# A hybrid decoder layer: 24 of its 32 gate blocks computed by seven block products in an early stage and kept in DRAM

## The chip, the cores and the metric

One NeuronCore of a Trainium2 chip runs the whole program in one launch. The metric is device time in microseconds of that core, the median of three runs. Engines are called PE (matmul; PEld its weight loads), DVE (vector), ACT (scalar, activations), POOL and SP (here only the queue that issues most DMAs).

## What is computed

A decoder layer on x of 1024 tokens by 1024 features, all in float32. After an RMSNorm, one projection feeds four mixers, each 512 wide: A (HGRN2), B (Mamba-2 SSD), C (GLA) and D (RG-LRU). They are merged with sigmoid gates, which are themselves projections of the normalised input:

```python
xn = rmsnorm(h, norm_mix_w[l]);  proj = xn @ w_in[l]          # mg: the last 4*1024 columns
yd = rglru_branch(lx, lg, ...)                               # conv, two gates, a scan, times gelu(lg)
branch_out = einsum('blnw,nwd->blnd', stack([ya, yb, yc, yd]), w_branch[l])
merged = sum(sigmoid(mg).reshape(b, s, 4, 1024) * branch_out, axis=2)
h = h + merged @ w_out[l]
g_ff, u_ff = split(rmsnorm(h, norm_ffn_w[l]) @ w_ffn_in[l], 2)
out = rmsnorm(h + (silu(g_ff) * u_ff) @ w_ffn_out[l], norm_f_w)
```

## The kernel before

Every float32 operand of a large matmul is split into a high part (type fp32r) and a remainder, and a product is three passes: high by high, high by low, low by high (`mm3`). ACT makes the high part (a cast) and DVE the remainder (a subtraction). The normalised input lies feature-major in `xn[hf][k]`: two token halves of 512, eight feature blocks of 128, each a pair of `half` tiles.

A projection block of 128 columns, `proj(col)`, loads 512 KB of weights, splits them (`load_w`, lines 151 and 152) and makes 8 x 3 matmuls of 512 columns for each token half, 48 in all. A gate block `gate(b, dm)` is such a projection with a tanh behind it (line 370). There are 32 of them, four branches b by eight blocks dm. `branch(b, dm)` multiplies the mixer's output with w_branch, 24 matmuls; DVE then forms (gate + 1) * branch (line 382, twice) and adds it into `merged[dm]` (line 386; not for branch 3, which comes first and whose g tile becomes `merged`). `merge(b, y)` does gate and branch for dm 0 to 7.

The program's order: norm and `split_fm` of both token halves (lines 231 to 235); RG-LRU (lines 425 to 471: projection LX, conv, small gate matmuls at line 431, sqrt at 456, scan at 460, projection LG with gelu at 348, the product at 468, the split of the result at 360 and 361); `values` for A (a token-major projection of 2 x 256 columns); hgrn(0); merge(3); A's four attentions with projections between them; merge(0); C's attention; the SSD, whose eight `chunk`s are called from merge(2), one ahead of each gate block; branch 1's eight gates in a row, then its eight branch products; w_out; the FFN. The FFN's input projection treats two blocks of 128 columns (a "pair") as a 2 x 2 block matrix and computes it by seven block products of 12 matmuls (84 for what would be 96) from sums of weight quarters S1 to S4 and of activation quarters T1 to T4 (lines 1034 to 1050, 1105 to 1108, 1116 to 1144; the T operands are made at lines 963 to 1013).

Large tiles (128 x 1024) come from a pool of 26, `slot`; halves (128 x 512) from a pool of 32, `half`. Weight staging: `wr` (raw), `wh`, `wl` have two buffers each; PSUM has 4 `pd`, 2 `pq` and 2 `pt` banks. A planner puts the instructions of each engine into one fixed order, by program order among those that its own model finds ready; on the chip each engine runs that order strictly. DMA issues of `nc.sync` stand in one such order on SP.

Of the kernel before, what the change touches and what calls it, by code (L numbers as in the profile page):

```python
# [38 lines left out]
P = 128  # L39
# [32 lines left out]
def trunk(ctx: ExitStack, tc: tile.TileContext, x, w_in, w_branch, w_out, w_fin, w_fout, prm_d, gw_d, lw_d,  # L72
# [43 lines left out]
    def f32(t):  # L116
        return t.bitcast(F32)
# [72 lines left out]
    def quad(p):  # L190
        return p.rearrange("p (c v) -> p c v", c=4)
# [30 lines left out]
            V.scalar_tensor_tensor(r, q, 1.5, r, op0=add, op1=mult)  # L222
        return r

    def split_fm(srcs, wcol, bank):

        res = []
        for k in range(KD):
            p = bank()
            for t in range(4):  # L230
                TE.transpose(p[:, t * P:(t + 1) * P], srcs[t][:, k * P:(k + 1) * P], ident)
            h, l = half(F32R), half(F32R)
            wc = pv(wcol, k)
            A.activation(h, p, AF.Copy, scale=wc)
            V.scalar_tensor_tensor(l, p, wc, f32(h), op0=mult, op1=sub)
            res.append((h, l))
            halves.append((h, l))
        return res

    halves = []  # L240

    def norm_x(hf):
        ss = sm.tile([P, 8], F32, name="ss", tag="ss")
# [19 lines left out]
    for hf in range(2):  # L263
        norm_x(hf)
        if hf == 0:
            wlx.append(load_w(None, KD, rlx[0]))
        xn[hf] = split_fm(xt[hf * 4:hf * 4 + 4], "nmix", allbank)
        if hf == 0:
# [12 lines left out]
    slot.free(*xt)  # L281

    def dense_fm(w, act, bank=dense_bank, first=None):

# [138 lines left out]
    cneg = cp.tile([P, 4], F32, name="cneg")  # L423
    rr, bb, th, yd = [], [], [], []
    for i in range(4):
        u = conv(proj(C_LX + i * P, *((wlx[i], first[i]) if i < 2 else ())), [pv("lcw", i * 4 + j) for j in range(4)], pv("lcb", i))
# [184 lines left out]
    def values(w):  # L611

        v = [slot() for _ in range(2)]

        def use(tp, p):
            for j in range(2):
                A.copy(tm(v[j])[:, tp * 2:tp * 2 + 2, :], p[:, :, j * P:(j + 1) * P])

        proj_tm(w, use)
        return v  # L620
# [325 lines left out]

    dp = ctx.enter_context(tc.tile_pool(name="dp", bufs=1, space=bass.MemoryType.DRAM))
# [3 lines left out]
    def two(dt=F32):  # L953
        t = slot(dt)
        return t[:, 0:H], t[:, H:T], t

    KH = KD // 2
    names = ("B11", "B21", "B22", "T1", "T2", "T3", "T4")
    ops = {n: [None] * KH for n in names}
    op_slots, op_halves = [], []  # L960
# [55 lines left out]
    class Pair:
        def __init__(self, j):
            self.j, self.W, self.held = j, {}, []
            graw = load_raw(w_fin[:, j * P:(j + 1) * P], KD)
            uraw = load_raw(w_fin[:, DFF + j * P:DFF + (j + 1) * P], KD)  # L1020
            g2, u2 = (a.rearrange("p (s k) n -> p s (k n)", s=2) for a in (graw, uraw))
            self.quads = g2[:, 0], g2[:, 1], u2[:, 0], u2[:, 1]
            gh, gl = whi(), wlo()
            graw = graw.rearrange("p k n -> p (k n)")
            A.copy(gh, graw)  # L1025
            V.tensor_sub(gl, graw, f32(gh))
            self.W["A11"], self.W["A12"] = (gh[:, 0:H], gl[:, 0:H]), (gh[:, H:T], gl[:, H:T])

        def sums(self, i):

            a11, a12, a21, a22 = self.quads
            x, h, l = slot(), slot(F32R), slot(F32R)
            if i == 0:
                V.tensor_add(x[:, 0:H], a21, a22)
                V.tensor_sub(x[:, H:T], x[:, 0:H], a11)
                self.s2 = x
            else:
                V.tensor_sub(x[:, 0:H], a11, a21)
                V.tensor_sub(x[:, H:T], a12, self.s2[:, H:T])
                slot.free(self.s2)  # L1040
            A.copy(h, x)
            V.tensor_sub(l, x, f32(h))
            for n, c in zip((("S1", "S2"), ("S3", "S4"))[i], (0, H)):
                self.W[n] = h[:, c:c + H], l[:, c:c + H]
            self.held += [h, l]
            if i:
                slot.free(x)
                uh, ul, ut = two(F32R)
                A.copy(uh, a22)
                V.tensor_sub(ul, a22, f32(uh))  # L1050
                self.W["A22"] = uh, ul
                self.held.append(ut)
# [45 lines left out]
    def ffn_in(j, early=False):  # L1098
# [1 line left out]
        pair = pairs.pop(j)  # L1100

        def product(p, a, b, first=True):
            ah, al = (t.rearrange("p (k n) -> p k n", k=KH) for t in pair.W[a])
            for k, (bh, bl) in enumerate(ops[b]):
                TE.matmul(p, lhsT=ah[:, k], rhs=bh, start=first and k == 0, stop=False, skip_group_check=True)  # L1105
                TE.matmul(p, lhsT=ah[:, k], rhs=bl, start=False, stop=False, skip_group_check=True)  # L1106
            for k, (bh, bl) in enumerate(ops[b]):
                TE.matmul(p, lhsT=al[:, k], rhs=bh, start=False, stop=k == KH - 1, skip_group_check=True)  # L1108
# [194 lines left out]
```

## Time and profile before

| | us |
|---|---|
| median of three runs (lowest, highest) | 2051.46 (2050.77, 2053.79) |
| the profiled execution: its own time | 2052.34 |
| its span, first to last instruction | 2050.4 |
| PE busy in the span | 2006.1 |
| DVE busy | 1030.5 |
| ACT busy | 632.9 |
| DMA traffic | 147.56 MB, mean 72 GB/s |

Busy time of PE counts matmuls that overlap in its pipeline, so a full PE is seen better in how many matmuls start per microsecond. The rows below show the stretches that the text speaks of.

### The profile page before, as it was taken

Reading aid. Unit: us, or ns where it says so; the run is one execution under the profiler, and the core shown is the slowest. Engines: PE = TensorE matmul, PEld = TensorE weight load, DVE = VectorE, ACT = ScalarE, POOL = GpSimd, SP = SyncE. Lnnn points to the kernel's source line nnn. Section 1 sums busy time; section 2 is a strip of 40 time slices with the busy share of each in tenths; the row PEclk is TensorE's granted clock in tenths of the full one; section 3 lists DMA queues with packets and bytes.
Section 4 is the critical chain, followed back from the end, with each engine's and each line's share of the span. In section 5 each row is a group of like instructions: output and inputs, shape, how many; then the busy total and the mean of one; then the engine's idle time right before and its main releaser. Section 6 shows DMA issues by size and latency. Waiting matters only on the chain.

```text
span 2050.4 us, 23991 instructions
## 1 busy us (share of the span) xinstructions
PE 2006.1 (98%) x9892; PEld 1663.1 (81%) x9892; DVE 1030.5 (50%) x1728; ACT 632.9 (31%) x942; POOL 14.2 (1%) x20
## 2 busy tenths in 40 slices
PE   7989999999999999999999999999999999999998
PEld 6779888889888878877779888877888888888886
DVE  6560114765242377566562517268665565554532
ACT  5742112332341111442122323154222232243421
POOL 0000000000000000000000000000000000000000
PEclk9999999999999999999999999999999999999999
DMA  5120111111112110111112014122222222466451
GB/s 172 31 72 11 51 52 32 29 46 42 32 32 61 41 32 21 42 42 31 31 43 66 21 52 154 52 93 83 91 64 93 93 64 91 128 205 221 154 165 41
DMA packets 157772, 147.56 MB, mean 72 GB/s; under 512 B 7472, under 2 KB 134880, under 8 KB 157664
## 3 DMA queue, kind: packets, MB, share of 16 engines
q1 hardware_dynamic: 153824, 136.82, 21.9%
q10 hardware_dynamic: 3840, 9.23, 1.2%
q8 instruction: 77, 1.26, 0.3%
q14 instruction: 31, 0.25, 0.0%
HBM read 126.10 MB, written 19.92 MB: 71 GB/s over the span
## 4 chain that ended last, share of the span: by engine, by line
PE 89%; DVE 7%; ACT 2%; issue 1%; DMA 1%; SPq 0%; DVEq 0%; ACTq 0%
PE pd L199 13%; PE pd L200 13%; PE pd L202 13%; PE pd L1106 3%; PE pd L1105 3%; PE pd L1108 3%; PE pd L318 3%; PE pd L316 3%; PE pd L317 3%; PE pd L1202 2%; PE pd L1203 2%; PE pd L1201 2%; PE pq L1108 2%; PE pq L1106 2%; PE pq L1105 2%; PE pt L1105 1%
## 5 line engine op out<-in xcount | busy, mean ns | idle before, releaser
L199 PE MATMUL pd<-x,wh 128*128 128x512 f32 x1056 | 420.1, 398 | 7.4 <-ACT s L348 7.0
L200 PE MATMUL pd<-x,wh 128*128 128x512 f32 x1056 | 418.1, 396 | 0.0
L152 DVE TENSOR_TENSOR wl<-wr,wh 128x1024 fp32r<-128x1024 f32 x82 | 100.4, 1224 | 370.8 <-PE pd L202 264.4
L202 PE MATMUL pd<-x,wl 128*128 128x512 f32 x1056 | 271.9, 394 | 0.0
L199 PEld LDWEIGHTS pd<-x,wh 128*128 128x128 f32 x1056 | 199.4, 189 | 51.8 <-ACT s L348 7.8
L200 PEld LDWEIGHTS pd<-x,wh 128*128 128x128 f32 x1056 | 199.4, 189 | 41.1 <-issue 2.4
L202 PEld LDWEIGHTS pd<-x,wl 128*128 128x128 f32 x1056 | 196.4, 188 | 42.8 <-issue 3.5
L151 ACT CAST wh<-wr 128x1024 fp32r<-128x1024 f32 x82 | 86.3, 1052 | 249.5 <-PE pd L200 227.8
L316 PE MATMUL pd<-s,x 128*128 128x256 f32 (+2 forms) x512 | 159.5, 312 | 0.6 <-ACT s L151 0.6
L318 PE MATMUL pd<-s,x 128*128 128x256 f32 (+2 forms) x512 | 159.8, 312 | 0.0
L317 PE MATMUL pd<-s,x 128*128 128x256 f32 (+2 forms) x512 | 159.6, 312 | 0.0
L370 ACT ACTIVATE s<-pd 128x512 f32<-128x512 f32 x64 | 38.3, 598 | 217.7 <-PE pd L202 217.7
L316 PEld LDWEIGHTS pd<-s,x 128*128 128x128 f32 x512 | 97.4, 190 | 5.7 <-ACT s L151 0.8
L317 PEld LDWEIGHTS pd<-s,x 128*128 128x128 f32 x512 | 97.5, 190 | 5.1
L318 PEld LDWEIGHTS pd<-s,x 128*128 128x128 f32 x512 | 97.5, 190 | 4.8
L199 PE MATMUL pd<-s,wh 128*128 128x512 f32 x256 | 99.8, 390 | 0.0
L200 PE MATMUL pd<-s,wh 128*128 128x512 f32 x256 | 99.8, 390 | 0.0
L382 DVE SCALAR_TENSOR_TENSOR s<-s,pd 128x512 f32<-128x512 f32 x64 | 43.9, 687 | 94.5 <-PE pd L202 94.5
L1159 DVE TENSOR_TENSOR s<-wr,s 128x1024 fp32r<-128x1024 f32 x44 | 53.9, 1225 | 69.0 <-ACT s L1158 54.2
L523 DVE COPY_PREDICATED s<-msk,pq 128x256 f32<-128x256 uint8 x128 | 61.9, 555 | 29.6 <-PE pq L517 16.2
L1025 ACT CAST wh<-wr 128x1024 fp32r<-128x1024 f32 x22 | 23.2, 1055 | 161.7 <-PE pq L1106 79.6
L202 PE MATMUL pd<-s,wl 128*128 128x512 f32 x256 | 68.5, 389 | 0.0
(341 smaller groups left out, 3560.4 us busy)
## 6 DMA issues: line engine op xcount, KB each, us to landing
wr<-in_w_in SPq DMA_DIRECT2D x76, 512.0 KB, 3.6
wr<-in_w_fin SPq DMA_DIRECT2D x44, 512.0 KB, 4.6
wr<-in_w_fout SPq DMA_DIRECT2D x44, 512.0 KB, 3.6
asp<-s SPq DMA_DIRECT2D x22, 512.0 KB, 4.9
x<-asp SPq DMA_DIRECT2D x42, 256.0 KB, 3.9
wr<-in_w_branch SPq DMA_DIRECT2D x16, 512.0 KB, 3.3
s<-in_x SPq DMA_DIRECT2D x8, 512.0 KB, 7.4
wr<-in_w_out SPq DMA_DIRECT2D x8, 512.0 KB, 3.9
```

The source lines that it names most:

```text
L151: i = A.copy(h, raw)
L152: V.tensor_sub(l, raw, f32(h))
L199: TE.matmul(p, lhsT=wh[k], rhs=ah, start=k == 0, stop=False)
L200: TE.matmul(p, lhsT=wh[k], rhs=al, start=False, stop=False)
L202: TE.matmul(p, lhsT=wl[k], rhs=ah, start=False, stop=k == n - 1)
L316: TE.matmul(p, lhsT=ah, rhs=wh, start=k == 0, stop=False)
L317: TE.matmul(p, lhsT=ah, rhs=wl, start=False, stop=False)
L318: TE.matmul(p, lhsT=al, rhs=wh, start=False, stop=k == n - 1)
L523: V.copy_predicated(dst[:, :, :, side, :], m, pv_[ab][:, i].rearrange("p c (n h) -> p c n h", h=h))
L1105: TE.matmul(p, lhsT=ah[:, k], rhs=bh, start=first and k == 0, stop=False, skip_group_check=True)
L1106: TE.matmul(p, lhsT=ah[:, k], rhs=bl, start=False, stop=False, skip_group_check=True)
L1108: TE.matmul(p, lhsT=al[:, k], rhs=bh, start=False, stop=k == KH - 1, skip_group_check=True)
```

## The change

Blocks of branch 3 (dm 0 to 7), branch 0 (dm 0 to 7), branch 2 (dm 4 to 7) and branch 1 (dm 4 to 7), 24 in all, are computed in a new stage `gates_phase` directly after `split_fm`, as 12 pairs by the FFN's scheme (class `Pair` and `block_product`, moved up and made general). Their tanh is stored to DRAM tiles `gsp`, and `gate` loads it from there. The stage also computes the four LX projections (kept in DRAM as `lxsp`) and makes the activation sums T1 to T4; `split_fm` of the second token half writes an unsplit copy of each feature block as well. Four feature blocks of the second half are given up during the stage (their unsplit copies lie in `xsp`), and are loaded and split again at its end. The RG-LRU comes after the stage and loads LX; A's two `values` calls stand between its blocks. `merge` may load up to three stored gates ahead while a slot is free.

```diff
 def split_fm(srcs, wcol, bank, raws=None):
             A.activation(h, p, AF.Copy, scale=wc)
             V.scalar_tensor_tensor(l, p, wc, f32(h), op0=mult, op1=sub)
+            if raws:
+                A.activation(raws[k], p, AF.Copy, scale=wc)
 def gate(b, dm):
         t = slot()
+        if (b, dm) in gsp:
+            nc.sync.dma_start(t, gsp[b, dm])
+            return t
 def merge(b, y, also=None):
+        gs = []
         for dm in range(KD):
             if also:
                 also(dm)
-            g = gate(b, dm)
+            while not gs or ((b, dm) in gsp and len(gs) < 3 and dm + len(gs) < KD and slot.held < slot.n):
+                gs.append(gate(b, dm + len(gs)))
             if dm % 2 == 0:
                 load_br(b, dm)
-            branch(b, dm, as_act(y), g, V)
+            branch(b, dm, as_act(y), gs.pop(0), V)
+    EARLY = ((3, 0), (0, 0), (2, 4), (1, 4))
+    gsp = {(b, dm): dp.tile([P, T], F32, ...) for b, dm0 in EARLY for dm in range(dm0, KD)}
+    def gates_phase():
+        def use(i, ps):
+            xx = in_order(ps)
+            nc.sync.dma_start(lxsp[i], xx)
+            slot.free(xx)
+        for i in range(2):
+            use(i, proj(0, wlx[i], first[i]))
+        ops = {"B11": xn[0][0:KH], "B21": xn[0][KH:], "B22": xn[1][KH:]}
+        left = [two() for k in range(KH)]
+        for k in range(KH):
+            nc.sync.dma_start(xsp[k], right[k][0])
+            V.tensor_add(b11, f32(h), f32(l))
+            V.tensor_sub(b11, b12, b11)
+            split("T1", k, b11)
+        use(2, proj(C_LX + 2 * P))
...
+        use(3, proj(C_LX + 3 * P))
+        prepare(0, 0)
...
+        for q in range(len(blocks) // 2):
+            prepare(q + 1, 0)
+            pair = pairs.pop(q)
+            pa, pb, pc, pd = (sbank(), tbank(), sbank(), tbank()) if q % 2 else (dense_bank() for i in range(4))
+            u = tmp()
+            g = [[half() for _ in range(2)] for _ in range(2)]
+            def done(i, hf, src):
+                A.activation(g[i][hf], src, AF.Tanh, scale=0.5)
+                nc.sync.dma_start(gsp[blocks[2 * q + i]][:, hs(hf)], g[i][hf])
+            product(pa, "A11", "B11")
+            A.copy(u, pa)
+            product(pd, "S1", "T1")
+            product(pb, "S2", "T2")
+            V.tensor_add(u, u, pb)
+            slot.free(*pair.held[0:2])
+            prepare(q + 1, 1)
+            product(pc, "S3", "T3")
+            V.tensor_add(g[1][1], u, pc)
+            V.tensor_add(g[1][1], g[1][1], pd)
+            done(1, 1, g[1][1])
+            product(pa, "A12", "B21", False)
+            done(0, 0, pa)
+            product(pc, "A22", "T4", False)
+            V.tensor_add(g[1][0], u, pc)
+            done(1, 0, g[1][0])
+            product(pd, "S4", "B22", False)
+            V.tensor_add(u, u, pd)
+            done(0, 1, u)
+        for k in range(KH):
+            r = tmp()
+            nc.sync.dma_start(r, xsp[k])
+            h, l = xn[1][k] = half(F32R), half(F32R)
+            A.copy(h, r)
+            V.tensor_sub(l, r, f32(h))
+    gates_phase()
     lw = slot()
     nc.scalar.dma_start(lw, lw_d)
+    wv = w_tm(C_HI)
+    va = []
     for i in range(4):
-        u = conv(proj(C_LX + i * P, ...), ...)
+        xx = slot()
+        nc.sync.dma_start(xx, lxsp[i])
+        u = conv(xx, ...)
...
         A.activation(th[i], r, AF.Tanh, scale=cpos[:, i:i + 1])
+        if i % 2 == 0:
+            va += values(wv)
+            if i == 0:
+                wv = w_tm(C_HI + 256)
...
-    va = []
-    for i in range(2):
-        w = wv
-        if i == 0:
-            wv = w_tm(C_HI + 256)
-        va += values(w)
     nxt = hgrn(0)
     merge(3, yd)
```

## Rows read from the trace of the kernel before

**Rows 1.** The page: span, and busy time of the engines with its share.

```profile
span 2050.4 us, 23991 instructions
PE 2006.1 (98%) x9892; PEld 1663.1 (81%) x9892; DVE 1030.5 (50%) x1728; ACT 632.9 (31%) x942; POOL 14.2 (1%) x20
```

**Rows 2.** Windows (start:end length, busy us per engine): merge(3), merge(0), FFN in, FFN out.

```profile
200.00:320.00 120.00, 120.00 (x531) 99.34 (x531) 23.48 (x27) 20.70 (x27) 0.00 (x0) 1.00 0.18 49
...
600.00:700.00 100.00, 100.00 (x443) 82.81 (x442) 26.55 (x28) 16.67 (x21) 0.00 (x0) 1.00 0.18 50
1400.00:1750.00 350.00, 350.00 (x1544) 289.76 (x1545) 218.63 (x292) 104.61 (x140) 0.00 (x0) 1.00 0.27 85
1800.00:1950.00 150.00, 150.00 (x663) 124.22 (x662) 76.31 (x112) 59.28 (x88) 0.00 (x0) 1.00 0.62 200
```

**Rows 3.** Chain that ended last, in time: one projection's two halves in merge(3).

```profile
240.55 1.81 PE pd L202 x8
245.99 1.81 PE pd L202 x8
```

**Rows 4.** Groups of DVE instructions in the FFN's input stage, 1400 to 1750.

```profile
L1042 DVE TENSOR_TENSOR s<-s 128x1024 fp32r<-128x1024 f32 x38 | 46.5, 1222 | 8.9 <-ACT s L1041 8.9
L1139 DVE TENSOR_TENSOR s<-s,t 128x512 f32<-128x512 f32 x19 | 13.1, 692 | 2.1 <-DVE t L1138 0.5
```

**Rows 5.** Windows at the end of the RG-LRU (columns as in Rows 2; then clock).

```profile
101.00:106.50 5.50, 3.79 (x17) 2.86 (x16) 5.50 (x5) 5.44 (x7) 0.00 (x0) 1.00 0.00 0
117.40:122.70 5.30, 0.05 (x1) 0.00 (x0) 4.19 (x5) 1.58 (x3) 0.00 (x0) 0.87 0.00 0
122.70:128.00 5.30, 5.29 (x13) 4.13 (x14) 4.19 (x6) 2.48 (x4) 0.00 (x0) 0.50 0.00 0
```

**Rows 6.** Timeline there: ACT and PE, with the idle time before each.

```profile
121.11 1.04 ACT L360 CAST s<-s 128x1024 fp32r<-128x1024 f32 x1 [9.48 <-DVE s L468]
...
122.71 0.80 PE L199 MATMUL pd<-x,wh 128*128 128x512 f32 x1 [5.26 <-ACT s L348]
```

**Rows 7.** Timeline of ACT in the second half's split_fm: first two of eight.

```profile
30.93 0.69 ACT L234 ACTIVATE x<-pt,prm 128x512 fp32r<-128x512 f32 x1 [3.54 <-PE pt L231]
31.52 0.68 ACT L234 ACTIVATE x<-pd,prm 128x512 fp32r<-128x512 f32 x1
```

**Rows 8.** Window in the FFN's operand preparation and first pairs.

```profile
1385.00:1395.00 10.00, 7.60 (x28) 4.52 (x27) 10.00 (x17) 3.07 (x6) 0.00 (x0) 1.00 0.00 1
```

**Rows 9.** DMA issues: KB of each, median us from issue to landing.

```profile
wr<-in_w_fout SPq DMA_DIRECT2D x44, 512.0 KB, 3.6
...
wr<-in_w_branch SPq DMA_DIRECT2D x16, 512.0 KB, 3.3
s<-in_x SPq DMA_DIRECT2D x8, 512.0 KB, 7.4
```

**Rows 10.** Timeline of DVE ahead of merge(0) and in it.

```profile
584.38 2.91 DVE L625 SCALAR_TENSOR_TENSOR s<-pt,prm,s 128x512 f32<-128x512 f32 x4
587.21 2.55 DVE L361 TENSOR_TENSOR s<-s 128x1024 fp32r<-128x1024 f32 x2
...
634.26 0.69 DVE L382 SCALAR_TENSOR_TENSOR s<-s,pd 128x512 f32<-128x512 f32 x1 [2.10 <-PE pd L202]
634.99 1.23 DVE L386 TENSOR_TENSOR s<-s 128x1024 f32<-128x1024 f32 x1
```

**Rows 11.** Windows of merge(2): chunks 4, 5, 6 with 7, the tail, one chunk.

```profile
1006.50:1029.30 22.80, 22.80 (x106) 17.10 (x105) 13.49 (x22) 3.69 (x6) 0.00 (x0) 1.00 0.16 47
1029.30:1052.10 22.80, 22.80 (x106) 17.24 (x105) 12.56 (x21) 4.30 (x6) 0.00 (x0) 1.00 0.08 24
1052.10:1075.20 23.10, 23.10 (x112) 16.65 (x111) 17.29 (x29) 6.62 (x10) 0.00 (x0) 1.00 0.17 46
1075.20:1097.00 21.80, 21.80 (x100) 18.09 (x99) 7.58 (x10) 3.19 (x4) 0.00 (x0) 1.00 0.17 49
...
961.00:976.00 15.00, 15.00 (x71) 10.90 (x72) 11.58 (x20) 1.97 (x4) 0.00 (x0) 1.00 0.13 35
```

More of the change, by code (lines that the diff above doesn't have):

```diff
@@ L223, in rstd_of, with split_fm @@
         return r
-    def split_fm(srcs, wcol, bank):
+    def split_fm(srcs, wcol, bank, raws=None):
         res = []
@@ L235, in split_fm, with two @@
             V.scalar_tensor_tensor(l, p, wc, f32(h), op0=mult, op1=sub)
+            if raws:
+                A.activation(raws[k], p, AF.Copy, scale=wc)
             res.append((h, l))
-            halves.append((h, l))
         return res
-    halves = []
+    dp = ctx.enter_context(tc.tile_pool(name="dp", bufs=1, space=bass.MemoryType.DRAM))
+    KH = KD // 2
+    def two(dt=F32):
+        t = slot(dt)
+        return t[:, 0:H], t[:, H:T], t
     def norm_x(hf):
@@ L266, in trunk @@
             wlx.append(load_w(None, KD, rlx[0]))
-        xn[hf] = split_fm(xt[hf * 4:hf * 4 + 4], "nmix", allbank)
-        if hf == 0:
+        if hf:
+            right = [two() for k in range(KH)]
+            xn[1] = split_fm(xt[4:8], "nmix", allbank, [right[k % KH][k // KH] for k in range(KD)])
+        else:
+            xn[0] = split_fm(xt[0:4], "nmix", allbank)
+            slot.free(*xt[0:4])
             wlx.append(load_w(None, KD, rlx[1]))
@@ L280, in trunk @@
     slot.free(mskf)
-    slot.free(*xt)
+    slot.free(*xt[4:8])
     def dense_fm(w, act, bank=dense_bank, first=None):
@@ L414, in conv, with __init__, sums @@
         return u
+    class Pair:
+        def __init__(self, w, c0, c1):
+            self.W, self.held = {}, []
+            graw = load_raw(w[:, c0:c0 + P], KD)
+            uraw = load_raw(w[:, c1:c1 + P], KD)
+            g2, u2 = (a.rearrange("p (s k) n -> p s (k n)", s=2) for a in (graw, uraw))
+            self.quads = g2[:, 0], g2[:, 1], u2[:, 0], u2[:, 1]
+            gh, gl = whi(), wlo()
+            graw = graw.rearrange("p k n -> p (k n)")
+            A.copy(gh, graw)
+            V.tensor_sub(gl, graw, f32(gh))
+            self.W["A11"], self.W["A12"] = (gh[:, 0:H], gl[:, 0:H]), (gh[:, H:T], gl[:, H:T])
+        def sums(self, i):
+            a11, a12, a21, a22 = self.quads
+            x, h, l = slot(), slot(F32R), slot(F32R)
+            if i == 0:
+                V.tensor_add(x[:, 0:H], a21, a22)
+                V.tensor_sub(x[:, H:T], x[:, 0:H], a11)
+                self.s2 = x
+            else:
+                V.tensor_sub(x[:, 0:H], a11, a21)
+                V.tensor_sub(x[:, H:T], a12, self.s2[:, H:T])
+                slot.free(self.s2)
+            A.copy(h, x)
+            V.tensor_sub(l, x, f32(h))
+            for n, c in zip((("S1", "S2"), ("S3", "S4"))[i], (0, H)):
+                self.W[n] = h[:, c:c + H], l[:, c:c + H]
+            self.held += [h, l]
+            if i:
+                slot.free(x)
+                uh, ul, ut = two(F32R)
+                A.copy(uh, a22)
+                V.tensor_sub(ul, a22, f32(uh))
+                self.W["A22"] = uh, ul
+                self.held.append(ut)
@@ new lines, in block_product @@
+    def block_product(pair, ops, p, a, b, first=True):
+        ah, al = (t.rearrange("p (k n) -> p k n", k=KH) for t in pair.W[a])
+        for k, (bh, bl) in enumerate(ops[b]):
+            TE.matmul(p, lhsT=ah[:, k], rhs=bh, start=first and k == 0, stop=False, skip_group_check=True)
+            TE.matmul(p, lhsT=ah[:, k], rhs=bl, start=False, stop=False, skip_group_check=True)
+        for k, (bh, bl) in enumerate(ops[b]):
+            TE.matmul(p, lhsT=al[:, k], rhs=bh, start=False, stop=k == KH - 1, skip_group_check=True)
@@ new lines, in trunk, with split, prepare, product @@
+    EARLY = ((3, 0), (0, 0), (2, 4), (1, 4))
+    gsp = {(b, dm): dp.tile([P, T], F32, name=f"gsp{b}_{dm}") for b, dm0 in EARLY for dm in range(dm0, KD)}
+    blocks = list(gsp)
+    lxsp = [dp.tile([P, T], F32, name=f"lxsp{i}") for i in range(4)]
+    xsp = [dp.tile([P, H], F32, name=f"xsp{i}") for i in range(KH)]
+    def gates_phase():
[6 more added lines that the diff above has]
+        ops = {"B11": xn[0][0:KH], "B21": xn[0][KH:], "B22": xn[1][KH:]}
+        ts = []
+        def split(n, k, src):
+            h, l, t = two(F32R)
+            A.copy(h, src)
+            V.tensor_sub(l, src, f32(h))
+            ops.setdefault(n, []).append((h, l))
+            ts.append(t)
+        left = [two() for k in range(KH)]
+        for k in range(KH):
+            nc.sync.dma_start(xsp[k], right[k][0])
+            (b11, b21, _), (b12, b22, _) = left[k], right[k]
+            h, l = xn[0][k]
+            V.tensor_add(b11, f32(h), f32(l))
[3 more added lines that the diff above has]
+        for k in range(KH):
+            (b11, b21, _), (b12, b22, _) = left[k], right[k]
+            V.tensor_sub(b12, b22, b12)
+            V.tensor_sub(b22, b22, b11)
+            split("T2", k, b22)
+        use(3, proj(C_LX + 3 * P))
+        pairs = {}
+        def prepare(q, i):
+            if 2 * q < len(blocks):
+                if i == 0:
+                    pairs[q] = Pair(w_in, *(C_MG + b * D + dm * P for b, dm in blocks[2 * q:2 * q + 2]))
+                pairs[q].sums(i)
+        prepare(0, 0)
+        for k in range(KH):
+            (b11, b21, lt), (b12, b22, rt) = left[k], right[k]
+            split("T3", k, b12)
+            h, l = xn[0][KH + k]
+            V.tensor_add(b21, f32(h), f32(l))
+            V.tensor_sub(b21, b21, b22)
+            slot.free(rt)
+        prepare(0, 1)
+        for k in range(KH):
+            split("T4", k, left[k][1])
+            slot.free(left[k][2])
+        for h, l in xn[1][0:KH]:
+            half.free(h, l)
+        for q in range(len(blocks) // 2):
[7 more added lines that the diff above has]
+                nc.sync.dma_start(gsp[blocks[2 * q + i]][:, hs(hf)], g[i][hf])
+            def product(p, a, b, first=True):
+                block_product(pair, ops, p, a, b, first)
+            product(pa, "A11", "B11")
[17 more added lines that the diff above has]
+            done(0, 1, u)
+            slot.free(*pair.held[2:])
+            half.free(*g[0], *g[1])
+        slot.free(*ts)
+        for k in range(KH):
+            r = tmp()
[3 more added lines that the diff above has]
+            V.tensor_sub(l, r, f32(h))
@@ L417, in trunk, with values, use @@
+    gates_phase()
+    def values(w):
+        v = [slot() for _ in range(2)]
+        def use(tp, p):
+            for j in range(2):
+                A.copy(tm(v[j])[:, tp * 2:tp * 2 + 2, :], p[:, :, j * P:(j + 1) * P])
+        proj_tm(w, use)
+        return v
     lw = slot()
     nc.scalar.dma_start(lw, lw_d)
+    wv = w_tm(C_HI)
+    va = []
     lwv = lw.rearrange("p (t g e) -> p t g e", t=4, g=2)
@@ L425, in trunk @@
     for i in range(4):
-        u = conv(proj(C_LX + i * P, *((wlx[i], first[i]) if i < 2 else ())), [pv("lcw", i * 4 + j) for j in range(4)], pv("lcb", i))
+        xx = slot()
+        nc.sync.dma_start(xx, lxsp[i])
+        u = conv(xx, [pv("lcw", i * 4 + j) for j in range(4)], pv("lcb", i))
         r, ig = slot(), slot()
@@ L609, in attention @@
         slot.free(st, *sT, *(Q if pair else [Q]))
[L611 to L620, printed above, removed]
     def gated(v, g, nw):
@@ L770, in sconv @@
     def sconv(i):
-        u = conv(proj(C_SX + i * P), [pv("scw", i * 4 + j) for j in range(4)], pv("scb", i))
+        u = conv(in_order(proj(C_SX + i * P)), [pv("scw", i * 4 + j) for j in range(4)], pv("scb", i))
         r = slot()
@@ L918, in trunk @@
     yb_act = [[tuple(a[:, hs(k % 2)] for a in yb[hf][k // 2]) for k in range(4)] for hf in range(2)]
-    for h, l in halves:
+    for h, l in xn[0] + xn[1]:
         half.free(h, l)
@@ L1013, in operands, with ffn_pair @@
             slot.free(left[k][2])
[L1016 to L1052, printed above, removed]
     pairs = {}
+    def ffn_pair(j):
+        return Pair(w_fin, j * P, DFF + j * P)
     def prepare(j):
         if j < NFF:
-            pairs[j] = Pair(j)
+            pairs[j] = ffn_pair(j)
             sums_of(j, 0)
@@ L1102, in product @@
         def product(p, a, b, first=True):
[L1103 to L1108, printed above, removed]
+            block_product(pair, ops, p, a, b, first)
         pa, pb, pc, pd = (sbank(), tbank(), sbank(), tbank()) if j % 2 else (dense_bank() for i in range(4))
```

14 lines of the change are left out of this document (5 added, 9 removed).

## The prediction

> **What bounds the kernel now.** I read the page first: PE is busy for 2006.1 of 2050.4 us, DVE for half of that [rows 1]. A busy PE can still be a slow one, so the windows come next: in merge(3), merge(0) and both FFN stages matmuls of 512 columns start at the same steady pace, 531 in 120 us, 443 in 100 us, 1544 in 350 us, while DVE works 20% to 62% of the time [rows 2]. The pace itself is read from the chain of waits: two halves of a projection, 24 matmuls each, end 5.44 us apart [rows 3], so one matmul costs 226.7 ns. PE's matmul count therefore sets the time almost everywhere, and every one taken off is worth 226.7 ns as long as something else doesn't leave PE waiting. The exceptions matter here: the end of the RG-LRU [rows 5, 6], and the preparation ahead of the FFN's pairs, where DVE is busy for 10.00 of 10 us and PE starts 28 matmuls instead of 44 [rows 8].
>
> **The seven products.** 24 gate blocks cost 24 x 48 = 1152 matmuls before, 12 x 84 = 1008 after: 144 fewer, 144 x 226.7 ns = 32.6 us. Whether the new stage keeps the pace is answered by its twin, the FFN's input stage: the same 84 matmuls in 19.04 us per pair, at full pace with DVE busy 218.63 of 350 us [rows 2], 11.9 us per pair. The gates' pair leaves out two half-width products of that (L1139 is such an operation, 0.69 us [rows 4]), so some 10.5 us of DVE in 19. The 24 weight loads are the same number as before; 48 stores of 256 KB come on SP's queue between them: per pair 1 MB in and 1 MB out, 2.1 MB in 19 us, 110 GB/s, where the FFN's output stage moves 200 at full pace [rows 2]. Behind a store that waits for its tanh stand only loads for a pair one further on. Pool `slot` reaches 25 of 26 in this stage by the code (16 for T1 to T4, 5 for a pair, up to 4 for the next), so this is tight, but each tile is needed 8 us or more after it comes free. I take the whole -32.6.
>
> **The start of the stage.** `split_fm` of the second half gets eight more ACT passes. ACT does one per 0.59 us in a row [rows 7], so the last block is split 8 x 0.59 = 4.7 us later. The first LX matmuls go through the blocks in order and need the last one 15 x 0.2267 = 3.4 us after the first. I take half of the delay, 2.5 us (between 0 and 4.7: no row tells how far ahead the splitting runs). T1 to T4 cost DVE 4 x (3 + 3 + 3 + 1) half-width operations = 40 x 0.69 = 28 us [rows 4], the first pair's sums and splits 7 more (three at 1.22, five at 0.69). Beside them PE has 144 matmuls of LX, 33 us, plus the first product. So DVE's 35 us lie just beside PE's 35: nothing, with a rival below for when they don't.
>
> **The RG-LRU.** At its end ACT waits 9.48 us for DVE's product behind the scans, the next gelu stands behind that cast on ACT, PE's banks stay full, and PE waits 5.26 us [rows 6]. It then runs at a granted clock of 0.50, so 1.2 instead of 2.4 GHz, for 5.3 us, 13 matmuls where 23 would fit [rows 5], a loss of 2.6 us; 1.7 us more are lost in 101 to 106.5 [rows 5]. Together 9.6 us. Now `values` (384 matmuls of half width, 44 us of PE by half the pace) stands between the blocks, so the first three blocks' sqrt and scan can be done before the last block's gates, and only one block's tail remains against 43 us of LG. I take 7 of the 9.6 back, because the join with the new stage (weights and LX loaded, four feature blocks split again) is new; between 0 and 9.6.
>
> **Merges without their gates.** A gate was 48 matmuls, 10.9 us of PE, beside which loads, splits and DVE were free. Left is the branch's 5.44 us per block.
> merge(3): 512 KB of gate and 256 KB of weights in 5.44 us is 145 GB/s; the FFN's output stage runs at 200 at full pace [rows 2], and up to three gates are loaded ahead. Nothing. yd's tail is covered by hgrn(0)'s 96 matmuls.
> merge(0), its start: the last gating ends at 587.29 and the last y split at 589.76 [rows 10], 2.5 us in which before a gate block ran; a branch can use three of its four blocks meanwhile (1.4 us). I take 2 (0 to 2.5).
> merge(0), its loop: slots held there are 8 `merged`, 8 of ya, 4 of vc, 4 of C's Q, K and F, 1 other F: 25 of 26. So one gate at a time: its load can only be issued when the add of the block before has read the only free slot, and the next add comes after the landing, two products and an add: 3.3, as for branch weights of the same size [rows 9], + 2 x 0.7 + 1.23 [rows 10] = 5.9 us. Every second block a branch weight load of 512 KB may run beside it, 2.6 us at 200 GB/s; if half of them meet, that is a quarter, 0.65, per block: 6.6 to PE's 5.44. Queued behind the waiting load on SP are those weight loads; they have a buffer to spare. PE has little to fill in, since attention needs slots too. Seven waits (the first gate is there early) of 1.14 are 8 us lost. Below, 0 (PE is the floor); above, a load that lands after 7.4 us as x's tiles do [rows 9] gives 10.0 per block, 7 x 4.6 = 32 us.
> merge(2), dm 4 to 7: chunks are DVE work, and the gate was what PE did beside it. From 1006.5 to 1097 PE is full for 90.5 us; without four gates (43.5) it would be 47. DVE's work there is 13.49 + 12.56 + 17.29 + 7.58 = 50.9 us [rows 11], less four weight splits of 1.22, 46. Both would have to be full at once, though chunk steps go to and fro between them: in the dense part of a chunk DVE is busy 11.58 of 15 us [rows 11]. Four chunks at 15 less the split, 13.5 each, 54, and about 3 for the last branch: 57 against 47. I take +10; between 0 and 4 x 15 + 10.6 (the tail without its gate) - 47 = 24.
> Branch 1's four stored gates are loaded behind four that PE still computes, 43.5 us: nothing.
>
> **The sum.** -32.6 + 2.5 - 7 + 2 + 8 + 10 = -17.1. The profiled execution took 2052.34 us, 0.9 above the median shown; 2035.2 on its scale is 2034 on the median's.
>
> **A rule against it.** In merge(0) PE would idle a microsecond per block. The row nearest to that, the FFN's start, shows the clock at 1.00 with PE idle 2.4 of 10 us in pieces [rows 8]; it fell to 0.50 only after 5.26 us without a matmul [rows 5, 6]. The Trainium skill, "TensorE: Matmul & The Clock Gate", section "HAM oscillation — how this bites in real kernels", says that a loop that waits for a DMA between groups of matmuls can lose its clock in each wait and start every group at half rate. By that rule merge(0)'s branch matmuls would run at half rate. This case's rows bear out the loss after a long wait, not after short ones. It is the fifth rival.
>
> **The rivals.**
> 1. Nothing is lost in the merges: loads land in time and the chunks overlap. Then -32.6 + 2.5 - 7 + 2 = -35: 2016. For it: DMA is at 0.18 in the merges [rows 2], and the planner may start chunks early. Against: the one free slot, and DVE's 46 us in 47.
> 2. The T operands don't fit beside LX: DVE at 10.00 of 10 in the FFN's own preparation [rows 8] speaks for it. If a quarter of the 35 us sticks out, 9 us: 2043.
> 3. Slower: merge(0)'s single slot meets slow loads. At 7.4 us a load [rows 9] 32 us are lost instead of 8: 2058. It decides from a loss of 25 there (8 + 17), a period of 5.44 + 25/7 = 9.0 us per block, a landing of 6.4 us. Against: the branch weights land after 3.3 [rows 9].
> 4. The change doesn't save what it should: with a pool one tile short of full, pairs wait for slots and take as long as 96 matmuls. 2034 + 32.6 = 2067. Against: the FFN's twin with a similar load [rows 2].
> 5. Half clock through merge(0): 192 x 226.7 ns = 43.5 more instead of 8: 2070.
>
> **Chances.** Forecast 0.52 (its own range 2022 to 2046), rivals 0.15, 0.13, 0.09, 0.08, 0.03. A change within 0.2%, 4 us, is about what this measurement cannot tell from none. Faster takes the forecast and the first two rivals but for a little at the upper end, 0.78; the same 0.06; slower 0.16. The range runs from the first rival's 2015 past the second's 2043 to 2050, where the costs in merge(0) and merge(2) come out 16 us above what I took.
>
> **What would show it.** Right: 84 matmuls in 19 us through the new stage, 12 times; no gap of 5 us and no clock of 0.50 at the LG projections; merge(0)'s adds 6 to 7 us apart, each released by a gate's DMA; chunks 4 to 7 some 13.5 us apart with DVE nearly full. Wrong: adds 5.44 us apart in merge(0), chunks 4 to 7 in under 50 us, pairs over 20 us, or PE waiting for T operands at the first pair.

## The result, and the profile after

The changed kernel takes 2017.99 us (median of four runs, 2017.31 to 2019.7), beside 2051.65 for the kernel before in the same comparison: a ratio of 0.9836, interval 0.9819 to 0.9853. It is faster by 33.7 us. The forecast was 2034 in 2015 to 2050: its direction held and the time lies in the range, but the gain is about twice the 17 us that the sum gave. The first rival, that nothing is lost in the merges, gave 2016 and came nearest; what its reason was worth is told under merge(2) and merge(0) below.

The page of the changed kernel, with the DMA rows of the gates' round trip through DRAM (KB of each, median us from issue to landing), answers to [rows 1, 9]:

```profile
span 2015.5 us, 24189 instructions
PE 1972.5 (98%) x9748; PEld 1636.4 (81%) x9748; DVE 1148.6 (57%) x1904; ACT 676.5 (34%) x1009; POOL 14.2 (1%) x20
...
gsp<-x SPq DMA_DIRECT2D x48, 256.0 KB, 2.0
s<-gsp SPq DMA_DIRECT2D x24, 512.0 KB, 4.4
```

PE has 144 matmuls fewer and DVE 118 us more, and PE's share is still 98%: the matmul count sets the time as before.

To see where the rest went, both spans are cut at the same PE instructions. The windows of the kernel before, at four of the cuts (start:end, length, busy us of PE, PEld, DVE, ACT, POOL with their instructions, granted clock, DMA share, GB/s): the start up to A's first attention score; from C's first low-rank matmul over A's end, merge(0) and C's operands to its cumulative sums; from the first `chunk` over merge(2) and the z projection to yb's transposes; and branch 1's stage up to the FFN's operands.

```profile
0.00:334.69 334.69, 313.89 (x1537) 261.32 (x1538) 124.67 (x151) 125.64 (x167) 3.06 (x8) 0.99 0.21 63
...
555.73:850.63 294.90, 289.66 (x1502) 239.37 (x1500) 145.04 (x271) 79.76 (x102) 7.51 (x8) 1.00 0.14 38
...
923.93:1142.66 218.73, 218.73 (x1179) 177.06 (x1179) 120.27 (x247) 47.84 (x83) 0.00 (x0) 1.00 0.14 40
1142.66:1344.32 201.66, 199.99 (x898) 165.12 (x897) 78.18 (x147) 51.87 (x86) 0.00 (x0) 1.00 0.23 76
```

The same four windows of the changed kernel:

```profile
0.00:470.18 470.18, 452.64 (x2161) 377.32 (x2162) 263.38 (x343) 202.22 (x280) 3.06 (x8) 1.00 0.35 112
...
691.69:903.09 211.40, 204.67 (x1118) 168.27 (x1117) 134.56 (x263) 61.73 (x78) 7.45 (x8) 0.99 0.18 53
...
976.47:1151.47 175.00, 174.95 (x987) 141.43 (x987) 114.98 (x243) 41.67 (x73) 0.00 (x0) 1.00 0.17 50
1151.47:1309.59 158.12, 156.46 (x707) 129.09 (x706) 73.27 (x143) 42.87 (x74) 0.00 (x0) 1.00 0.28 97
```

Each stage's change is set against its change in matmuls at 226.7 ns [rows 3]; what is left is what the stage lost or won beside the count.

| stage | length, us | matmuls | at 226.7 ns | left | forecast of it |
|---|---|---|---|---|---|
| start to merge(3) | +135.5 | +1008 - 384 | +141.5 | -6.0 | +2.5 - 7 = -4.5 |
| A's end, merge(0), C's operands | -83.5 | -384 | -87.1 | +3.6 | +2 + 8 = +10 |
| chunks, merge(2), z | -43.7 | -192 | -43.5 | -0.2 | +10 |
| branch 1 | -43.5 | -192 | -43.5 | 0.0 | 0 |
| the other four | +0.4 | 0 | 0 | +0.4 | 0 |
| sum | -34.9 | -144 | -32.6 | -2.3 | +15.5 |

The last column against the one before it is the whole of the forecast's error, 17.8 us: 10.2 of them lie in the chunks, 6.4 in merge(0), 1.5 in the front part.

### The profile page after: what moved, and what is told of

It is laid out like the page before. It is cut to its first block, busy times and chain, and to the rows that moved or that the text cites. A ratio compares the mean times of both kernels' runs of the same rounds, so it can differ in the third digit from the quotient of the medians.

```text
span 2015.5 us, 24189 instructions
## 1 busy us (share of the span) xinstructions
PE 1972.5 (98%) x9748; PEld 1636.4 (81%) x9748; DVE 1148.6 (57%) x1904; ACT 676.5 (34%) x1009; POOL 14.2 (1%) x20
## 4 chain that ended last, share of the span: by engine, by line
PE 90%; DVE 6%; ACT 2%; issue 1%; DMA 1%; SPq 0%; DVEq 0%; ACTq 0%
PE pd L200 10%; PE pd L199 9%; PE pd L202 9%; PE pd L478 5%; PE pd L477 5%; PE pd L480 5%; PE pq L480 3%; PE pq L478 3%; PE pq L477 3%; PE pd L328 3%; PE pd L326 3%; PE pd L327 3%; PE pt L477 2%; PE pt L480 2%; PE pt L478 2%; PE pd L1331 2%
## 5 line engine op out<-in xcount | busy, mean ns | idle before, releaser
L199 PE MATMUL pd<-x,wh 128*128 128x512 f32 x672 | 269.9, 402 | 2.8 <-DVE s L395 2.2
L200 PE MATMUL pd<-x,wh 128*128 128x512 f32 x672 | 267.7, 398 | 0.0
L202 PE MATMUL pd<-x,wl 128*128 128x512 f32 x672 | 173.3, 394 | 0.0
L152 DVE TENSOR_TENSOR wl<-wr,wh 128x1024 fp32r<-128x1024 f32 x58 | 70.9, 1225 | 142.6 <-PE pd L202 99.7
L199 PEld LDWEIGHTS pd<-x,wh 128*128 128x128 f32 x672 | 127.5, 190 | 29.7 <-issue 4.3
L200 PEld LDWEIGHTS pd<-x,wh 128*128 128x128 f32 x672 | 127.6, 190 | 25.5 <-issue 1.3
L202 PEld LDWEIGHTS pd<-x,wl 128*128 128x128 f32 x672 | 124.9, 188 | 25.8 <-issue 0.8
L151 ACT CAST wh<-wr 128x1024 fp32r<-128x1024 f32 x58 | 61.0, 1052 | 223.4 <-PE pd L200 208.8
L461 ACT CAST s<-s 128x1024 fp32r<-128x1024 f32 x68 | 71.6, 1053 | 110.9 <-DVE s L455 74.3
L462 DVE TENSOR_TENSOR s<-s 128x1024 fp32r<-128x1024 f32 x68 | 83.2, 1223 | 21.9 <-ACT s L461 21.9
L478 PE MATMUL pd<-s 128*128 128x512 f32 x228 | 89.3, 392 | 2.0 <-DVE s L1138 2.0
L477 PE MATMUL pd<-s 128*128 128x512 f32 x228 | 89.2, 391 | 1.7 <-ACT s L1137 1.7
L445 ACT CAST wh<-wr 128x1024 fp32r<-128x1024 f32 x34 | 35.7, 1049 | 162.6 <-PE pq L478 79.6
```

Source lines behind the costliest of these rows:

```text
L152: V.tensor_sub(l, raw, f32(h))
L199: TE.matmul(p, lhsT=wh[k], rhs=ah, start=k == 0, stop=False)
L200: TE.matmul(p, lhsT=wh[k], rhs=al, start=False, stop=False)
L202: TE.matmul(p, lhsT=wl[k], rhs=ah, start=False, stop=k == n - 1)
```

## The experiments

Ratios are to the kernel before, run on the same chip (2051.8 to 2052.0 us there), with 95% intervals. "The change" is the kernel with the whole change. Stages are cut as above.

**The z projection held back.** In the forecast, chunks 4 to 7 leave PE 10 us short. The first three of these windows of the changed kernel begin with chunks 4, 5 and 6, the last with the first matmul of the z projection, 3 us ahead of chunk 7. The chunks start 12.6, 13.8 and 16.7 us apart, where the forecast had 13.5:

```profile
1059.00:1071.60 12.60, 12.60 (x61) 8.94 (x60) 10.05 (x17) 1.49 (x3) 0.00 (x0) 1.00 0.25 85
1071.60:1085.40 13.80, 13.80 (x67) 9.87 (x65) 11.21 (x21) 1.20 (x2) 0.00 (x0) 1.00 0.12 38
1085.40:1099.00 13.60, 13.60 (x65) 10.23 (x64) 10.72 (x20) 3.30 (x4) 0.00 (x0) 1.00 0.13 41
1099.00:1116.00 17.00, 16.95 (x122) 14.61 (x121) 15.80 (x25) 9.66 (x10) 0.00 (x0) 1.00 0.62 167
```

Yet PE is full in each. The groups of PE instructions in the last window show with what: 89 matmuls of 256 columns at lines 326 to 328, which are the SSD's z projection. In the dense stretches of the timeline they start 0.12 us apart, so 89 x 0.12 = 10.7 us.

```profile
L326 PE MATMUL pd<-s,x 128*128 128x256 f32 x30 | 8.7, 291 | 0.0
L327 PE MATMUL pd<-s,x 128*128 128x256 f32 x30 | 8.6, 286 | 0.0
L328 PE MATMUL pd<-s,x 128*128 128x256 f32 x29 | 8.4, 289 | 0.0
```

In the experiment a one-column copy that reads the last chunk's result stands ahead of the split of z's weights, so that z can't start before the chunk ends.

```diff
-    def wide(*srcs):
+    def wide(*srcs, behind=None):
...
+            if behind is not None:
+                A.copy(h[:, 0:1], behind)
...
-            wz.append(w_tm(C_SZ))
+            wz.append(wide(w_in[:, C_SZ:C_SZ + 256], behind=Xv[3][:, 1, 0:1]))
```

> The weights of the SSD's z projection wait for the last chunk's result, so z can't run beside the chunks. Theory (DVE paces chunks 4 to 7 as forecast, and z's first matmuls are what PE does meanwhile): the 10.4 us of z that ran before the last chunk's end come behind it, with up to 2.3 us for the late cast and split: 2028 to 2031 us. Rival (the chunks don't need a filler, their steps overlap by themselves): 2018 to 2020 us.

Measured: 2026.62 us, 0.9878 [0.9863, 0.9893], 1.4 us below the theory's band and well above the rival's. The stage takes 183.6 instead of 175.0 us, and the last window is now, in this kernel:

```profile
1099.00:1116.00 17.00, 11.85 (x49) 7.89 (x48) 14.96 (x24) 3.57 (x6) 0.00 (x0) 0.74 0.00 0
```

PE is busy 11.85 of 17 us, and its clock falls. Of the 10 us in the span 8.6 lie in this stage. The other 1.4 are in the front part, where kernels differ by as much without an edit there: the one with two places for the gates (below) takes 1.3 more.

How large the hole is without z is read from this kernel's timelines, chunk 4's first matmul, the last chunk's last sum and z's first matmul, and from the window of z's start (lines stand two further on in this kernel):

```profile
1060.62 0.48 PE L1003 MATMUL pt<-s 64*128 64x128 f32 x2
...
1111.64 0.68 DVE L1031 TENSOR_TENSOR s<-s,t 128x512 f32<-128x512 f32 x1
...
1113.68 1.22 PE L328 MATMUL pd<-s,x 128*128 128x256 f32 x4 [3.28 <-ACT s L151]
...
1113.60:1117.40 3.80, 3.68 (x16) 3.39 (x17) 2.39 (x2) 1.16 (x3) 0.00 (x0) 0.51 0.35 102
```

The last four chunks take 1112.3 - 1060.6 = 51.7 us, against the 47 of PE's own work: a hole of about 5 us. Another 1.4 pass until z's late weights are cast, which is the edit's own cost, and z then starts at half clock: its first 15 matmuls take 3.7 us, where 0.12 us each would be 1.8, a loss of about 2. So the hole is real, about half of the forecast's 10 us, and in the change the z projection fills it.

**Without branch 2's early gates.** The list of early gates loses `(2, 4)`, so 20 gate blocks in 10 pairs are computed early.

```diff
-    EARLY = ((3, 0), (0, 0), (2, 4), (1, 4))
+    EARLY = ((3, 0), (0, 0), (1, 4))
```

> Branch 2's four blocks go back into merge(2) as plain gates; 20 blocks, 10 pairs, stay early. Theory (removing them from merge(2) cost nothing): 24 matmuls more, 24 x 226.7 ns = 5.4 us slower, 2023.4 us. The forecast's term (10 us lost in merge(2)): 5.4 - 10 = 4.6 us faster, 2013.4 us.

Measured: 2026.94 us, 0.9878 [0.9863, 0.9893], 3.5 above the theory's 2023.4; the span is 7.5 us over the change's, on the theory's side of zero. The stage of the chunks takes 218.69 us, 43.7 more for 192 matmuls (43.5): moving branch 2's gates costs this stage nothing. Two pairs less mean 24 matmuls more, 5.4 us; the other 2 lie in the front part, which takes 434.03 us where two pairs less would be 470.18 - 168 x 0.2267 = 432.1, again by the size of such differences there.

**A's values behind the RG-LRU.** The new place of `values` is undone; all else stays.

```diff
-    wv = w_tm(C_HI)
-    va = []
     for i in range(4):
...
-        if i % 2 == 0:
-            va += values(wv)
-            if i == 0:
-                wv = w_tm(C_HI + 256)
...
+        if i == 3:
+            wv = w_tm(C_HI)
...
+    va = []
+    for i in range(2):
+        w = wv
+        if i == 0:
+            wv = w_tm(C_HI + 256)
+        va += values(w)
```

> A's two value projections go back behind the LG projections, as in the kernel before; all else as in the change. Theory (these projections between the RG-LRU's blocks are what covers its sqrt and scan tail): at least the 9.6 us of stall and half clock come back, and the LX projections that stood there before are missing too: 2028 to 2038 us. Rival (the tail shrank because LX and its weights left the stage): 2018 to 2020 us.

Measured: 2047.98 us, 0.9981 [0.9972, 0.9991], nearly all of the gain gone; the front part takes 502.4 us, 32.2 more than in the change. The direction is the theory's, the size was missed. Windows of this kernel within the RG-LRU:

```profile
340.00:360.00 20.00, 6.14 (x8) 2.28 (x8) 13.85 (x13) 13.62 (x14) 0.00 (x0) 0.62 0.00 0
360.00:380.00 20.00, 14.26 (x53) 11.28 (x54) 18.89 (x15) 9.42 (x11) 0.00 (x0) 0.84 0.00 0
```

PE starts 8 matmuls in 20 us, and the clock is at 0.62. The expectation took the kernel before as the measure of this stall; there the four LX projections (192 matmuls, 43.5 us) stood between the RG-LRU's blocks, and here they have gone into the new stage. So taking LX out opens the hole, and `values` fills it. That is read from the order of the program: LX back in its old place was not tried.

**The unsplit copies on DVE.** The eight ACT passes in `split_fm` are replaced by eight DVE sums of the high and the low part. The copies then hold that sum and not the product itself.

```diff
-            xn[1] = split_fm(xt[4:8], "nmix", allbank, [right[k % KH][k // KH] for k in range(KD)])
+            xn[1] = split_fm(xt[4:8], "nmix", allbank)
+            for k in range(KD):
+                V.tensor_add(right[k % KH][k // KH], f32(xn[1][k][0]), f32(xn[1][k][1]))
```

> The unsplit copies of the second half's feature blocks are made by DVE from high part plus remainder, not by ACT from PSUM. Theory (eight more ACT passes, and the PSUM banks they hold, delay the first LX matmuls by 5 us): 2013 to 2015 us. Rival (DVE is the short one in the operands' preparation, 5.5 us more of it come out at the first pair): 2018 to 2023 us.

Measured: 2012.51 us, 0.9809 [0.9793, 0.9825]. The front part takes 466.8 instead of 470.2 us. At the start of the stage, windows of the changed kernel and then PE's timeline there, with the idle time before each instruction and its releaser:

```profile
31.90:36.90 5.00, 1.35 (x10) 0.88 (x9) 2.71 (x4) 5.00 (x10) 0.00 (x0) 1.00 0.49 189
36.90:42.00 5.10, 5.10 (x16) 4.03 (x17) 4.23 (x7) 3.20 (x6) 0.00 (x0) 0.67 0.05 20
```

```profile
32.81 0.66 PE L231 MATMUL pd<-cst,s 128*128 128x128 f32 x4 [0.91 <-ACT s L237]
...
35.70 0.66 PE L231 MATMUL pd<-cst,s 128*128 128x128 f32 x4 [2.24 <-ACT s L237]
...
36.86 0.50 PE L199 MATMUL pd<-x,wh 128*128 128x512 f32 x1 [0.50 <-ACT s L237]
```

PE waits for the added ACT pass (line 237) ahead of two groups of transposes and of the first matmul, since that pass reads the PSUM bank that the next of them writes, and then runs part of 5 us at half clock. The same windows with the copies on DVE:

```profile
31.90:36.90 5.00, 3.64 (x22) 2.62 (x21) 5.00 (x8) 4.25 (x8) 0.00 (x0) 1.00 0.00 0
36.90:42.00 5.10, 5.10 (x24) 4.24 (x23) 5.10 (x9) 1.64 (x2) 0.00 (x0) 1.00 0.53 206
```

The windows count 46 matmuls and transposes in place of 26, at the full clock. Of the 5.7 us in the span, 3.4 lie in the front part and are the edit's. Another 1.6 lie in the stage of merge(0), which the edit doesn't touch: the half clock at its end did not come in this kernel (see merge(0) below). That takes the time below the theory's band. The experiment's rival, that DVE is the short engine here, falls.

**Two places for merge(0)'s gates.** Every second gate of branch 0 is loaded in halves into two tiles of another pool, so that its load need not wait for the one free slot.

```diff
+        if b == 0 and dm % 2:
+            t = [tmp(), tmp()]
+            for hf in range(2):
+                nc.sync.dma_start(t[hf], gsp[b, dm][:, hs(hf)])
+            return t
...
+        if isinstance(g, list):
+            for hf in range(2):
+                V.scalar_tensor_tensor(g[hf], g[hf], 1.0, ps[hf], op0=add, op1=mult)
+                eng.tensor_add(merged[dm][:, hs(hf)], merged[dm][:, hs(hf)], g[hf])
+            return
...
-            while not gs or ((b, dm) in gsp and ...):
+            while not gs or (b == 0 and len(gs) < 2 and dm + 1 < KD) or ((b, dm) in gsp and ...):
```

> In merge(0) every second stored gate is loaded into two half-width work tiles, so the next gate's load no longer waits for the add of the block before. Theory (the one free slot costs the 3.5 us that this stage lost): 2014 to 2015 us. Rival (the stage's loss is that attention's steps slip between merge(0)'s on DVE): 2018 us, as with the change.

Measured: 2013.79 us, 0.9816 [0.9801, 0.9831]. The stage takes 207.9 instead of 211.4 us; by count alone it would be 294.9 - 87.1 = 207.8. So the single slot costs 3.5 us, the whole of what merge(0) had lost; part of that is half clock behind a wait, and where the clock held it is less: 209.8 us with the copies on DVE, 207.5 with both mends below, so 2.3. In windows of the stretch in which PE is busy least, the changed kernel first:

```profile
750.00:775.00 25.00, 22.20 (x98) 17.99 (x97) 15.80 (x21) 2.10 (x2) 3.96 (x5) 0.93 0.41 126
```

and with the second place:

```profile
750.00:775.00 25.00, 24.34 (x123) 20.18 (x122) 19.62 (x30) 2.11 (x2) 4.72 (x5) 1.00 0.21 63
```

**All of branch 1's gates early.** Two more pairs, 28 blocks in all.

```diff
-    EARLY = ((3, 0), (0, 0), (2, 4), (1, 4))
+    EARLY = ((3, 0), (0, 0), (2, 4), (1, 0))
```

> All eight gates of branch 1 early, 28 blocks in 14 pairs. Saved: 24 matmuls, 5.4 us. Theory (branch 1's four plain gates are what PE does beside the SSD's last normalisation and split, 34 of their matmuls, 7.7 us): 5.4 saved, 7 to 8 lost, 2019 to 2021 us. Rival (nothing lost): 2012.6 us.

Measured: 2022.28 us, 0.9856 [0.984, 0.9872], slower than the change by 4.3, a microsecond beyond the theory's band. Branch 1's stage takes 123.45 us, where 192 matmuls fewer would leave 158.12 - 43.5 = 114.6: 8.9 lost for 5.4 saved. A window of this kernel at the stage's start shows where:

```profile
1190.00:1200.00 10.00, 5.38 (x30) 4.33 (x29) 9.23 (x47) 4.87 (x17) 0.00 (x0) 0.83 0.96 355
```

PE is busy 5.38 of 10 us. Its longest wait in the stage, by the view of waits (us in total, times, longest), is the one of yb's transposes for DVE:

```profile
PE pt L1082 <- DVE s L1087: 4.2, 1, 4.2
```

The gates that PE still computes in branch 1 of the change are the cover of yb's last steps.

**All of branch 2's gates early.** The same with the other branch.

```diff
-    EARLY = ((3, 0), (0, 0), (2, 4), (1, 4))
+    EARLY = ((3, 0), (0, 0), (2, 0), (1, 4))
```

> All eight gates of branch 2 early, 28 blocks. Saved: 5.4 us. Theory (DVE paces a chunk at 12.6 to 14 us, PE's own work for one is 12; the z projection can fill 10 us at the end only, which the last four chunks use already): 5.4 saved, 3 to 10 lost, 2016 to 2023 us. Rival (chunks overlap): 2012.6 us.

Measured: 2047.11 us, 0.9976 [0.9966, 0.9985]. The stage takes 165.3 us where 192 matmuls fewer would leave 131.5: 33.8 lost, over three times what was expected at most. In windows of this kernel a chunk takes 13 us where the clock is full, and later the clock is not:

```profile
1075.00:1088.00 13.00, 12.08 (x58) 8.10 (x54) 10.03 (x20) 1.20 (x2) 0.00 (x0) 1.00 0.12 42
...
1110.00:1120.00 10.00, 7.47 (x22) 4.92 (x22) 6.58 (x12) 4.40 (x5) 0.00 (x0) 0.50 0.39 110
1120.00:1130.00 10.00, 7.09 (x24) 5.05 (x24) 9.02 (x16) 0.60 (x1) 0.00 (x0) 0.50 0.39 107
```

Without gates eight chunks of 13.5 us pace the stage, and on top of that the clock is at half in stretches, so that PE's own steps between DVE's take twice as long. How the 33.8 us divide between the two was not measured.

**Both mends together.** The copies on DVE and the second place for merge(0)'s gates.

> Both edits in one: unsplit copies by DVE (measured 2012.5 alone) and the second gate buffer in merge(0). If the two are independent and the buffer gains its 3.5 us: 2009 us; if the buffer gains nothing: 2012.5 us.

Measured: 2009.01 us (2008.62 to 2009.3), 0.979 [0.9775, 0.9805], the fastest of all: 9.0 below the change and 43.0 below the kernel before (2052.03 beside it). The front part takes 466.9 us and the stage of merge(0) 207.5: the two gains add, 3.3 + 3.9 of the span's 8.4. Of the 3.9, 1.6 had come with the copies on DVE alone.

## Why the forecast's direction was right and its size not

**The seven products: right.** -32.6 us. In windows of the changed kernel, the twelve pairs, the RG-LRU and merge(3):

```profile
71.20:299.80 228.60, 228.60 (x1010) 189.12 (x1009) 126.30 (x161) 81.11 (x113) 0.00 (x0) 1.00 0.40 124
299.80:359.20 59.40, 58.06 (x414) 51.24 (x412) 28.34 (x30) 37.04 (x55) 0.00 (x0) 1.00 0.24 74
359.20:470.20 111.00, 111.00 (x487) 91.04 (x486) 56.84 (x66) 43.79 (x50) 1.44 (x2) 1.00 0.25 81
```

228.6 / 12 = 19.05 us per pair, the FFN's 19.04 [rows 2], with PE never idle; DVE is busy 126.3 / 12 = 10.5 us per pair, as worked out. The fourth rival, pairs that wait for slots, falls; 124 GB/s stand beside the forecast's 110. So does the second, T operands that don't fit: PE waits for none of them at the first pair.

**The start: the place right, the size not.** Taken at +2.5, in a range of 0 to 4.7. The delay was counted as ACT's time alone; the added pass also keeps the PSUM bank from the next transpose, and the waits cost clock. In the kernel before PE's only wait here is

```profile
34.43 0.50 PE L199 MATMUL pd<-x,wh 128*128 128x512 f32 x1 [0.48 <-DVE x L235]
```

In the change the three waits shown above are 3.65 us, and a mean clock of 0.67 over 5.1 us costs a third of them, 1.7: by these rows the start cost some 4.9 us, at the top of the range. Moving the passes to DVE gave back 3.4 of it; what the eight sums on DVE cost in their place was not measured.

**The RG-LRU: right, the size a little low.** Taken at -7 of 9.6. The second window above holds `values` and the small gate matmuls, and PE is idle there for 1.3 us of 59.4 at the full clock. The third begins with the LG projections, where the kernel before had its stall, and goes through hgrn(0) and merge(3): PE is busy 111.00 of 111 us at a clock of 1.00. So of [rows 5, 6] nothing is left, no wait of 5 us and no 0.50, and 9.6 - 1.3 = 8.3 us came back. The front part as a whole came out at -6.0; with 3.4 to 4.9 lost at the start, that would make it 9.4 to 10.9. The two ways differ by about as much as kernels without an edit there do (1.3 and 1.4 us, above). That `values` is the cover is shown: without it the front part is 32 us longer.

**merge(3), branch 1: right.** Taken at nothing; merge(3) is full in the third window, branch 1's stage came out at 0.0. The experiment with all of branch 1 shows how close that is: four more gates moved and 8.9 us appear.

**merge(0): DVE's loop right, PE's waits mis-sized.** Taken at 2 + 8, it cost 3.6. DVE's timeline in merge(0), the answer to [rows 10]:

```profile
729.49 1.28 DVE L395 SCALAR_TENSOR_TENSOR s<-s,pd 128x512 f32<-128x512 f32 x2 [3.41 <-DMA s<-gsp]
730.81 1.23 DVE L399 TENSOR_TENSOR s<-s 128x1024 f32<-128x1024 f32 x1
...
741.22 1.29 DVE L395 SCALAR_TENSOR_TENSOR s<-s,pd 128x512 f32<-128x512 f32 x2 [3.41 <-DMA s<-gsp]
742.54 1.23 DVE L399 TENSOR_TENSOR s<-s 128x1024 f32<-128x1024 f32 x1
```

The first five products wait for their gate's DMA, which lands some 3.4 us after it is issued, behind the add before; the first gate's too, which the forecast had as early. The adds come 5.8 to 6.0 us apart where nothing else is in between, the 5.9 of the forecast before the surcharge of 0.65 for weight loads that meet the gate's; that surcharge didn't show.

What the forecast had wrong is that PE would wait as often as DVE ("Seven waits"). A window of the merge's first 40 us, then PE's timeline behind it, with the window after its longest wait:

```profile
719.70:759.90 40.20, 40.03 (x182) 32.47 (x181) 21.83 (x25) 5.29 (x6) 0.00 (x0) 1.00 0.41 127
...
762.16 0.50 PE L199 MATMUL pd<-s,wh 128*128 128x512 f32 x1 [0.55 <-DVE s L395]
...
770.15 0.47 PE L199 MATMUL pd<-x,wh 128*128 128x512 f32 x1 [2.25 <-DVE s L395]
...
771.00:774.60 3.60, 3.60 (x11) 2.77 (x10) 3.60 (x6) 0.00 (x0) 0.00 (x0) 0.53 0.44 130
```

PE makes the branch's matmuls one behind the other while DVE falls back by half a microsecond per block: the products wait in the four `pd` banks, two blocks' worth. Only the last block finds no free bank, 0.55 us, and then the next projection, 2.25 us. Behind that wait eight matmuls start 0.42 us apart, at half clock, 1.6 us more. The stage's other waits are 1.3 us shorter than before. The start of the merge, taken at 2, cost PE 0.16 us.

The third rival's loads of 7.4 us did not come: the gate loads land after 4.4 in the median, 3.4 in this loop.

**merge(2): the step that failed.** "Four chunks at 15 less the split, 13.5 each, 54, and about 3 for the last branch: 57 against 47. I take +10." Two things were wrong with it. The 47 was not what stood against the 57: it counted only PE's work up to the end of the merge, and the next work in program order, the z projection, depends on nothing in the chunks. Its 10.7 us of matmuls moved into the hole, so the stage lost nothing. And the hole was taken too large: with z held back the chunks took 51.7 us, 52.8 to the merge's last add, not 57, and the 8.6 us that this cost are some 5 of hole, 2 of half clock and 1.4 of the edit's own. So the first rival's reason, that the chunks overlap with what PE has left, holds about half way, and z does the rest. A stage's hole is a loss only if no later work may enter it, and the forecast didn't look at what came next.

**The rule against it.** The fifth rival, half clock through merge(0), did not come: the clock is 1.00 there up to its last block and 0.53 for 3.6 us behind its end. The forecast was right about it by luck: PE does not wait in that loop, so the rule was not put to the test, and the reason that the forecast gave, that the loss follows a long wait and not short ones, fell as well; see the last section.

## What to carry to other kernels

When work is taken out from beside a slow chain, the loss is not the chain's length less the work that is left in its stage: first look at what stands next in the order and waits for nothing in the chain. Such cover is used up once, though: moving four more gates out of either branch lost more (8.9 and 33.8 us) than their products save (5.4). And a move that opens a hole belongs with one that fills it: with `values` left in its old place, all but 4 us of the gain were gone.

## What the runs showed of the hardware that was not expected

The granted clock fell to its lower level (0.50, 1.2 GHz) without a long wait ahead of it. In the kernel with all of branch 2 early, the longest wait of PE from 1098 to 1130 is 2.8 us, by its waits (us in total, times, longest):

```profile
PE pt L1010 <- DVE t L1008: 4.6, 2, 2.8
```

and the clock is 0.50 in 1110 to 1130 (windows above). In the changed kernel it was 0.67 over 36.9 to 42, behind waits of 0.91, 2.24 and 0.50 us in which PE was busy 1.35 of 5 us; with z held back it was 0.74 in 1099 to 1116. In the kernel before only a wait of 5.26 us had shown it [rows 5, 6], and 7.60 of 10 us busy had kept it [rows 8].

Nor does the same wait always cost it. The 2.25 us at the end of merge(0), behind 0.55 us a block earlier, stand in the kernel with the copies on DVE as well, and the clock stays at 1.00:

```profile
766.21 0.47 PE L199 MATMUL pd<-x,wh 128*128 128x512 f32 x1 [2.25 <-DVE s L397]
...
767.20:770.80 3.60, 3.60 (x22) 3.11 (x20) 3.60 (x6) 0.00 (x0) 0.06 (x1) 1.00 0.38 115
```

That is the 1.6 us by which this kernel's stage is shorter. The kernel without branch 2's early gates keeps its clock there too; those with z held back and with all of branch 2 early lose it.

The Trainium skill, "TensorE: Matmul & The Clock Gate", section "HAM oscillation — how this bites in real kernels", says that a loop that idles between groups of matmuls can lose its clock again and again. The kernel with all of branch 2 early agrees, with 0.50 in pieces. merge(0) neither agrees nor disagrees: it is DVE that waits for a DMA in each block, and PE is busy 40.03 of 40.20 us. What decides whether a wait of about 2 us costs the clock in these runs was not tried.
